# A hybrid decoder layer in float32: a zero-padded bias table, so that bias and row minimum of the attention scores take one instruction instead of two

## The chip, the core and the metric

The kernel runs on one core of a Trainium2 chip. The core has five engines that work side by side, each through a queue of its own: PE (TensorE, matrix products; PEld is its weight load), DVE (VectorE), ACT (ScalarE), POOL (GpSimd) and SP (SyncE, which here issues the transfers). The data lie in SBUF, products of PE land in PSUM. The metric is the device time of one execution in microseconds (us); less is better.

## The reference, cut to what matters

One layer over 1024 positions of 1024 numbers: a norm, one input projection, four mixers side by side (pooling, a short gated convolution, a Conformer convolution, differential attention), an output projection, then a norm and a SwiGLU block of width 2816. The change lies in the attention, which has 4 heads and two maps for each head:

```python
def block(args):
    qblk, start = args
    qpos = start + jnp.arange(Q_BLOCK, dtype=jnp.int32)      # Q_BLOCK = 128
    dist = qpos[:, None] - kpos[None, :]
    bias = rel_bias[rel_bucket(jnp.maximum(dist, 0))]        # 32 buckets
    sc = einsum('bqhmd,bkhmd->bhmqk', qblk, k) * scale + bias
    sc = jnp.where(dist >= 0, sc, NEG_INF)
    p = jax.nn.softmax(sc, axis=-1)
    a = p[:, :, 0] - lam * p[:, :, 1]
    return jnp.einsum('bhqk,bkhd->bqhd', a, v)
```

The bias depends on the distance alone, and from 128 positions back on it is one constant for each head. A constant drops out of the softmax. So only the last 256 columns of a block of 128 rows need a bias (and the mask), measured from that constant; further back it is zero.

## The kernel before, in words

Everything is float32. A product is taken as three matmuls of a high and a low part (mm3, L138 to L140). The program runs through these stages: norm and transpose of x, the input projection with the convolutions on DVE (until about 165 us), projections of K, Q and V (until about 246 us), the scores with the attention (246 to about 400 us), the second norm, and the gate, up and down products to the end.

The attention goes over four pairs of row blocks, p = 0 to 3, and in each over four heads (`unit`). A pair has two blocks i of 128 rows; block i of pair p sees w = 128(2p+1+i) columns, so w runs from 128 to 1024. For each block and each of the two maps m:

- PE writes the negated scores to PSUM, `sc` (L673).
- If w is over 256, DVE takes the minimum over the first w-256 columns into `fmx` (L680). These columns have no bias.
- DVE adds the bias table `tb` to the last 256 columns in place and takes their minimum, with `fmx` as the value to start from, into `mx` (L681, a custom instruction, and a short one that reads its accumulator).
- ACT takes the exponential of mx minus all w columns into `pt`, with the row sums (L684).
- When both maps are there, DVE combines them (L686 to L688).

Then PE transposes the result by blocks into `tp` (L699), ACT and DVE evict it as a high and a low part `at` (L703, L704), and PE multiplies it by V (L708). Other matmuls, those of the output projection for the other mixers (`fm`, L604 to L606), are handed out into gaps of this work by a list of counts (FQ), one entry at each call of `fill1`. Their weights `wo` come through `wsplit`: load, cast to the high part on ACT (L120), low part on POOL (L134).

`tb` (128 x 4 heads x 256) is computed once, from PSUM by two copies on ACT (L461). Its buffer serves again for weights of the gate and up products (`tb2`, loaded by L970).

The order on each engine is not the order of the text: when the program is built, a planner with its own estimates of cost orders the instructions of each engine, by priority and by what is ready. `issue_after` fixes single pairs.

Of the kernel before, what the change touches and what calls it, by code (L numbers as in the profile page):

```python
# [11 lines left out]
F = mybir.dt.float32  # L12
R = mybir.dt.float32r
AF = mybir.ActivationFunctionType
ALU = mybir.AluOpType
AX = mybir.AxisListType
# [3 lines left out]
P = 128  # L20
# [46 lines left out]
def tile_hybrid(ctx, tc, x, norm1_g, w_in, pool_w, pool_scale, sconv_w, conf_w, conf_b, ln_g, ln_b,  # L67
# [3 lines left out]
    V, A, G, T = nc.vector, nc.scalar, nc.gpsimd, nc.tensor  # L71
    dma = nc.sync.dma_start
    x, out, w_in, w_out = x[0], out[0], w_in[0], w_out[0]
# [9 lines left out]
    def pool(name, bufs=1, side="left", **kw):  # L83
        return tc.tile_pool(name=name, bufs=bufs, side=side, reuse_waits="tile", **kw)
# [33 lines left out]
    def cp(e, dst, src):  # L118
        if e == 0:
            A.copy(dst, src)  # L120
        else:
            (V, G)[e - 1].tensor_copy(dst, src)
# [119 lines left out]
    for p in range(4):  # L242
# [16 lines left out]
        h = p // 2  # L259
# [106 lines left out]
    tb = const.tile([P, 4, 256], F, name="tb")  # L366
# [102 lines left out]
    kvp = mid.enter_context(pool("kvp"))  # L469
    VV = [kvp.tile([P, 2, 4, 128], R, name=f"VV{p}") for p in range(4)]  # L470
    qn = [kvp.tile([P, 2, 256], F, name=f"qn{p}") for p in range(4)]

    def proj_tok(c0, use, order=range(4)):
        Ws = [wsplit(w_in[k * 512:(k + 1) * 512, c0:c0 + 256].rearrange("(k p) c -> p k c", p=P), (4,))
              for k in range(2)]
        for p in order:
            ps = ps_mm()
            H = hT[p // 2]
            for i in range(2):
                c = (p % 2) * 256 + i * P  # L480
                o = ps[:, i * 256:(i + 1) * 256]
                for kt in range(8):
                    W = Ws[kt // 4]
                    mm3(o, (H[0][:, kt, c:c + P], H[1][:, kt, c:c + P]), (W[0][:, kt % 4], W[1][:, kt % 4]), kt == 0, kt == 7)
            use(p, ps)
# [99 lines left out]
    def ps_sc():  # L585
        return pss.tile([P, 1024], F, name="sc", tag="sc")

    def ps_tp():
        return psp.tile([P, 512], F, name="tp", tag="tp")

    def ps_av():
        return psq.tile([P, 512], F, name="av", tag="av")
# [48 lines left out]
    def fill1(ins, n=None):  # L641
        for _ in range(next(slots, 0) if n is None else n):
            while fillq:
                f = next(fillq[0], None)
                if f is not None:
                    if GATE:
                        with tc.issue_after(ins.ins):
                            f()
                    else:
                        f()  # L650
                    break
                fillq.pop(0)
# [4 lines left out]
    def unit(u, p, h):  # L657
        if h == 0:
            pend["lt"] = sm.tile([P, 4, 2, 2], F, name="lt", tag="lt", bufs=2)
            pend["o"] = sm.tile([P, 2, 4, 64], F, name="o", tag="kn")  # L660
        lt, o = pend["lt"], pend["o"]
        Ps = []
        for i in range(2):
            w = P * (2 * p + 1 + i)
            nw = min(w, 256)
            pts = [None, None]
            both = ps_sc() if p < 2 else None
            for m in MO:
                hm = 2 * h + m
                sc = ps_sc() if both is None else both[:, 512 * m:512 * m + 512]  # L670
                for c0 in range(0, w, 512):
                    n = min(max(w - c0, 256), 512)
                    ins = T.matmul(sc[:, c0:c0 + n], lhsT=QT[p, h // 2][:, hm % 4, i * P:(i + 1) * P],  # L673
                                   rhs=KT[h // 2][:, hm % 4, c0:c0 + n], start=True, stop=True)
                fill1(ins)
                mx = sm.tile([P, 1], F, name="mx", tag="mx", bufs=4)
                init = 3.0e38
                if w > 256:
                    init = sm.tile([P, 1], F, name="fmx", tag="fmx", bufs=2)
                    V.tensor_reduce(init, sc[:, 0:w - 256], axis=AX.X, op=ALU.min)  # L680
                V.tensor_tensor_reduce(out=sc[:, w - nw:w], in0=sc[:, w - nw:w], in1=tb[:, h, 256 - nw:], scale=1.0,  # L681
                                       scalar=init, op0=ALU.add, op1=ALU.min, accum_out=mx)
                pts[m] = ap4.tile([P, S], F, name="pt", tag=f"pt{m}", bufs=PT1 if m else PT0)
                A.activation(pts[m][:, 0:w], sc[:, 0:w], AF.Exp, bias=mx, scale=-1.0, accum_out=lt[:, h, m, i:i + 1])  # L684
            cf = sm.tile([P, 1], F, name="cf", tag="cf", bufs=4)
            V.reciprocal(cf, lt[:, h, 1, i:i + 1])  # L686
            V.scalar_tensor_tensor(cf, lt[:, h, 0, i:i + 1], nlam, cf, op0=ALU.mult, op1=ALU.mult)
            V.scalar_tensor_tensor(pts[0][:, 0:w], pts[1][:, 0:w], cf, pts[0][:, 0:w], op0=ALU.mult, op1=ALU.add)  # L688
            Ps.append(pts[0])
        if h % 2 == 0:  # L690
            pend["av"] = ps_av()
        avs = pend["av"]
        av = avs[:, (h % 2) * 256:(h % 2) * 256 + 256]
        for kb in range(p + 1):
            ps = ps_tp()
            blocks = [(a, i) for a in range(2) for i in range(2) if 2 * kb + a <= 2 * p + i]
            nb = len(blocks) * P
            for j, (a, i) in enumerate(blocks):
                ins = T.transpose(ps[:, j * P:(j + 1) * P], Ps[i][:, (2 * kb + a) * P:(2 * kb + a + 1) * P], ident)  # L699
            marks.append(ins)  # L700
            fill1(ins)
            at = ap4.tile([P, 2, 512], R, name="at", tag="at", bufs=ATB)
            A.copy(at[:, 0, 0:nb], ps[:, 0:nb])  # L703
            V.tensor_tensor(at[:, 1, 0:nb], ps[:, 0:nb], at[:, 0, 0:nb].bitcast(F), op=ALU.subtract)  # L704
            for s in range(2):
                for a in range(2):
                    n = min(nb - 256 * a, 256)
                    ins = T.matmul(av[:, 256 - n:256], lhsT=VV[kb][:, a, h, :], rhs=at[:, s, 256 * a:256 * a + n],  # L708
                                   start=(kb == 0 and a == 0 and s == 0), stop=(kb == p and a == 1 and s == 1))
                if s == 0:  # L710
                    fill1(ins)
        marks.append(ins)
        fill1(ins)
        if h % 2 == 1:
            oT = sm.tile([P, 512], F, name="oT", tag="sq")
            cp(OTE[u // 2], oT, avs)
            ps = ps_tp()
            for hh in range(2):
                for i in range(2):
                    ins = T.transpose(ps[:, (i * 2 + hh) * P:(i * 2 + hh + 1) * P], oT[:, hh * 256 + i * P:hh * 256 + (i + 1) * P], ident)  # L720
            marks.append(ins)
            fill1(ins)
            psv = ps.rearrange("p (i h d) -> p i h d", i=2, h=2)
            ov = o[:, :, h - 1:h + 1, :]
            cp(OVE[u // 2], ov, psv[:, :, :, 64:128])
            V.tensor_tensor(ov, ov, psv[:, :, :, 0:64], op=ALU.add)
        if h == 3:
            of = o.rearrange("p i h d -> p (i h) d")
            osq = sm.tile([P, 8, 64], F, name="osq", tag="sq")
            A.activation(osq, of, AF.Square)  # L730
            rr = sm.tile([P, 2, 4], F, name="rr", tag="rr", bufs=2)
            rrf = rr.rearrange("p i h -> p (i h)")
            V.tensor_reduce(rrf, osq, axis=AX.X, op=ALU.add)
            l0 = lt[:, :, 0, :]
            l2 = sm.tile([P, 4, 2], F, name="l2", tag="l2", bufs=2)
            V.scalar_tensor_tensor(l2, l0, EPS, l0, op0=ALU.mult, op1=ALU.mult)
            V.scalar_tensor_tensor(rr, rr, 1.0 / 64, l2.rearrange("p h i -> p i h"), op0=ALU.mult, op1=ALU.add)
            G.tensor_tensor(rrf, rrf, mhalf[:, 0:8], op=ALU.pow)
            (G if X5[PO.index(p)] else V).tensor_tensor(qn[p].rearrange("p i (h d) -> p (i h) d", h=4), of, rrf.unsqueeze(2).broadcast_to([P, 8, 64]),
                            op=ALU.mult)  # L740
# [85 lines left out]
    for u in range(16):  # L826
        j, h = u // 4, u % 4
        p = PO[j]
# [355 lines left out]
```

## Time and profile before

| | |
|---|---|
| median of 3 runs | 1082.94 us (1082.12 to 1084.14) |
| the profiled execution: its time, its span | 1081.06 us, 1079.3 us |
| PE busy | 1051.2 us, 97% of the span |
| DVE busy | 732.8 us, 68% |
| ACT busy | 438.9 us, 41% |
| POOL busy | 222.5 us, 21% |
| granted clock of TensorE | 1.000 of full speed |

The span runs from the first to the last instruction. Busy shares are means over the span; what an engine's time is worth differs from stage to stage. A matmul's duration in the trace includes its way through the pipeline, so a PE that is busy all of the time isn't one without any slack.

### The profile page before, as it was taken

How to read it: one execution, taken by the hardware profiler on the slowest of the kernel's cores; microseconds unless marked ns; L12 is line 12 of the kernel's file. 1: busy time of each engine (PE TensorE's matmuls, PEld its weight loads, DVE VectorE, ACT ScalarE, POOL GpSimd, SP SyncE). 2: the span in 40 equal slices, each digit the busy share in tenths (PEclk: the TensorE clock that was granted, in tenths of full speed). 3: DMA queues.
4: the chain of work that ended last, by engine and by line, in shares of the span. 5: the costliest groups of instructions: out<-in, count | busy, mean ns of one | idle time of the engine just before them, and what ended most of it. 6: DMA issues, size and time to landing. Idle time of an engine off the chain costs nothing.

```text
span 1079.3 us, 13508 instructions
## 1 busy us (share of the span) xinstructions
PE 1051.2 (97%) x5203; PEld 875.7 (81%) x5203; DVE 732.8 (68%) x1127; ACT 438.9 (41%) x710; POOL 222.5 (21%) x202
## 2 busy tenths in 40 slices
PE   7999999998989999899999999999999999999998
PEld 7878879996778876788878888888888888888886
DVE  5599984657899966888677675556656567555541
ACT  5512124545786766432332333333333244333320
POOL 5137114655676653000000000000000000000000
PEclk9999999999999999999999999999999999999999
DMA  8131210111021121014576663233223268766721
GB/s 216 49 98 40 59 39 20 40 40 40 30 71 47 50 81 37 14 54 154 210 280 244 250 208 108 73 112 127 88 79 127 106 228 296 246 195 214 231 101 39
DMA packets 89664, 128.04 MB, mean 119 GB/s; under 512 B 17112, under 2 KB 57600, under 8 KB 87040
## 3 DMA queue, kind: packets, MB, share of 16 engines
q1 hardware_dynamic: 89600, 127.18, 36.0%
q8 instruction: 41, 0.67, 0.3%
q14 instruction: 23, 0.19, 0.1%
HBM read 94.13 MB, written 33.04 MB: 118 GB/s over the span
## 4 chain that ended last, share of the span: by engine, by line
PE 81%; DVE 9%; DMA 5%; ACT 2%; issue 1%; POOL 1%; SPq 0%; ACTq 0%; DVEq 0%; POOLq 0%
PE sb L140 10%; PE sb L138 10%; PE sb L139 10%; PE mm L138 6%; PE mm L139 6%; PE mm L140 6%; PE dx L140 3%; PE dx L138 3%; PE dx L139 3%; PE dy L140 3%; PE dy L138 3%; PE dy L139 3%; DMA wd<-in_w_down_dram 2%; DMA dT<-wd 2%; PE fm L606 1%; PE fm L604 1%
## 5 line engine op out<-in xcount | busy, mean ns | idle before, releaser
L138 PE MATMUL sb<-T,rhi 128*128 128x512 f32 x320 | 125.6, 392 | 0.0
L140 PE MATMUL sb<-T,rlo 128*128 128x512 f32 x320 | 125.5, 393 | 0.0
L139 PE MATMUL sb<-T,rhi 128*128 128x512 f32 x320 | 125.5, 392 | 0.0
L911 DVE TENSOR_TENSOR dq<-ds,dq 128x2048 fp32r<-128x2048 f32 x35 | 80.1, 2291 | 60.3 <-ACT dq L910 60.1
L910 ACT CAST dq<-ds 128x2048 fp32r<-128x2048 f32 x35 | 66.8, 1910 | 105.5 <-PE dy L140 39.6
L134 POOL TENSOR_TENSOR wlo<-st,whi 128x1024 fp32r<-128x1024 f32 (+2 forms) x30 | 73.4, 2449 | 113.0 <-ACT whi L120 101.9
L138 PE MATMUL mm<-hT,whi 128*128 128x512 f32 (+1 forms) x224 | 81.0, 373 | 2.4 <-ACT whi L120 1.9
L139 PE MATMUL mm<-hT,whi 128*128 128x512 f32 (+1 forms) x224 | 82.8, 373 | 0.3 <-DVE hT L200 0.2
L140 PE MATMUL mm<-hT,wlo 128*128 128x512 f32 (+1 forms) x224 | 82.1, 370 | 0.0
L317 DVE SCALAR_TENSOR_TENSOR t<-u,cw,t 128x1023 f32<-128x1023 f32 (+28 forms) x58 | 71.4, 1267 | 0.7
L138 PEld LDWEIGHTS sb<-T,rhi 128*128 128x128 f32 x320 | 60.1, 188 | 13.7 <-DVE tp L1030 0.4
L139 PEld LDWEIGHTS sb<-T,rhi 128*128 128x128 f32 x320 | 60.1, 188 | 13.5
L140 PEld LDWEIGHTS sb<-T,rlo 128*128 128x128 f32 x320 | 60.1, 188 | 13.5
L910 ACT CAST rhi<-st 128x1024 fp32r<-128x1024 f32 x28 | 29.4, 1051 | 85.2 <-PE sb L139 46.5
L140 PE MATMUL dx<-dq 128*128 128x512 f32 x160 | 62.4, 390 | 0.0
L139 PE MATMUL dx<-dq 128*128 128x512 f32 x160 | 62.3, 389 | 0.0
L138 PE MATMUL dx<-dq 128*128 128x512 f32 x160 | 61.9, 390 | 0.0
L684 ACT ACTIVATE pt<-sc,mx 128x128 f32<-128x128 f32 (+7 forms) x64 | 47.6, 747 | 18.2 <-DVE mx L681 18.2
L138 PE MATMUL mm<-whi,hT 128*128 128x256 f32 x192 | 54.8, 288 | 0.0
L139 PE MATMUL mm<-wlo,hT 128*128 128x256 f32 x192 | 54.5, 285 | 0.0
L140 PE MATMUL mm<-whi,hT 128*128 128x256 f32 x192 | 54.4, 284 | 0.0
L120 ACT CAST whi<-st 128x1024 fp32r<-128x1024 f32 x28 | 29.4, 1050 | 58.8 <-PE mm L139 52.8
(342 smaller groups left out, 2683.6 us busy)
## 6 DMA issues: line engine op xcount, KB each, us to landing
ds<-dL SPq DMA_DIRECT2D x35, 512.0 KB, 4.0
wd<-in_w_down_dram SPq DMA_DIRECT2D x10, 1024.0 KB, 5.0
dT<-wd SPq DMA_DIRECT2D x10, 1024.0 KB, 4.0
dL<-afs SPq DMA_DIRECT2D x10, 1024.0 KB, 4.4
ds<-dT SPq DMA_DIRECT2D x20, 512.0 KB, 5.4
st<-in_w_in_dram SPq DMA_DIRECT2D x18, 512.0 KB, 3.7
st<-in_w_gate_dram SPq DMA_DIRECT2D x15, 512.0 KB, 4.0
st<-in_w_up_dram SPq DMA_DIRECT2D x15, 512.0 KB, 3.6
```

Of the source, the lines that this page charges most:

```text
L120: A.copy(dst, src)
L134: G.tensor_tensor(lo[:, nv:], st[:, nv:], hi[:, nv:].bitcast(F), op=ALU.subtract)
L138: T.matmul(ps, lhsT=L[0], rhs=Rr[0], start=first, stop=False, skip_group_check=more)
L139: T.matmul(ps, lhsT=L[0], rhs=Rr[1], start=False, stop=False, skip_group_check=more)
L140: return T.matmul(ps, lhsT=L[1], rhs=Rr[0], start=False, stop=last, skip_group_check=more)
L317: V.scalar_tensor_tensor((z if s == 30 else acc)[:, s:], u[:, :S - s], w[:, 30 - s:31 - s], acc[:, s:], op0=ALU.mult, op1=ALU.add)
L604: yield lambda: T.matmul(ps, lhsT=L[0], rhs=Rr[0], start=first, stop=False)
L606: yield lambda: T.matmul(ps, lhsT=L[1], rhs=Rr[0], start=False, stop=last)
L684: A.activation(pts[m][:, 0:w], sc[:, 0:w], AF.Exp, bias=mx, scale=-1.0, accum_out=lt[:, h, m, i:i + 1])
L910: A.copy(hi, src)
L911: (eng or V).tensor_tensor(lo, src, hi.bitcast(F), op=ALU.subtract)
```

## The change

A wider table `tbw` of 7 blocks of 128 columns for each head is made: blocks 0 to 4 are zero (cleared by POOL), blocks 5 and 6 are a copy of `tb` (by ACT). It is laid out by block, then head, then column. Now up to 896 columns take bias and minimum in one instruction. At w = 384 to 896 no L680 is left; at w = 1024 it goes over the first 128 columns. Lines of the changed kernel from here on stand three further down, and then four.

```diff
     qn = [kvp.tile([P, 2, 256], F, name=f"qn{p}") for p in range(4)]
+    tbw = kvp.tile([P, 7, 4, 128], F, name="tbw")
+    G.memset(tbw[:, 0:5], 0.0)
+    A.copy(tbw[:, 5:7].rearrange("p b h n -> p h b n"), tb.rearrange("p h (b n) -> p h b n", b=2))
...
             w = P * (2 * p + 1 + i)
-            nw = min(w, 256)
+            nw = min(w, 896)
...
-                if w > 256:
+                if w > nw:
                     init = sm.tile([P, 1], F, name="fmx", tag="fmx", bufs=2)
-                    V.tensor_reduce(init, sc[:, 0:w - 256], axis=AX.X, op=ALU.min)
-                V.tensor_tensor_reduce(out=sc[:, w - nw:w], in0=sc[:, w - nw:w], in1=tb[:, h, 256 - nw:], scale=1.0,
+                    V.tensor_reduce(init, sc[:, 0:w - nw], axis=AX.X, op=ALU.min)
+                scv = sc[:, w - nw:w].rearrange("p (b n) -> p b n", n=P)
+                V.tensor_tensor_reduce(out=scv, in0=scv, in1=tbw[:, 7 - nw // P:, h, :], scale=1.0,
                                        scalar=init, op0=ALU.add, op1=ALU.min, accum_out=mx)
```

## Rows read from the trace of the kernel before

**Rows 1.** Busy time by stretch: us, then each engine (instructions), clock, DMA

```profile
170.00:180.00 10.00, 10.00 (x87) 10.00 (x86) 4.62 (x11) 4.05 (x9) 3.21 (x2) 1.00 0.01 2
...
280.00:300.00 20.00, 18.39 (x105) 14.85 (x103) 17.73 (x59) 15.22 (x42) 13.53 (x17) 1.00 0.10 31
300.00:320.00 20.00, 17.67 (x104) 14.68 (x102) 19.40 (x47) 16.40 (x37) 13.98 (x13) 1.00 0.21 65
...
340.00:360.00 20.00, 20.00 (x112) 17.35 (x111) 17.90 (x38) 13.20 (x26) 12.98 (x17) 1.00 0.14 41
```

**Rows 2.** Waits from 246 to 410 us: total us, times, longest

```profile
ACT pt L684 <- DVE mx L681: 18.2, 22, 2.1
...
PEld av L708 <- DVE at L704: 5.1, 8, 1.5
```

**Rows 3.** Chain that ended last, from 266 to 340 us: start, us, piece

```profile
279.20 0.53 DVE fmx L680 x2
279.73 0.40 DVE sc L681
...
305.09 1.10 DVE fmx L680 x2
306.18 0.40 DVE sc L681
...
314.65 0.60 DVE fmx L680
```

**Rows 4.** DVE's instructions by line and shape: count, busy, mean ns

```profile
L681 DVE CUSTOM_DVE_ANT_0 sc<-sc,tb,fmx 128x256 f32<-128x256 f32 x48 | 22.4, 485 | 0.1
...
L704 DVE TENSOR_TENSOR at<-tp,at 128x512 fp32r<-128x512 f32 x24 | 16.3, 683 | 3.9 <-ACT at L703 3.9
...
L704 DVE TENSOR_TENSOR at<-tp,at 128x384 fp32r<-128x384 f32 x16 | 8.8, 551 | 2.7 <-ACT at L703 2.7
...
L726 DVE TENSOR_TENSOR o<-o,tp 128x256 f32<-128x256 f32 x8 | 3.3, 414 | 0.0
```

**Rows 5.** DVE in order of time: start us, duration us, line, instruction

```profile
264.37 0.29 DVE L681 CUSTOM_DVE_ANT_0 sc<-sc,tb 128x128 f32<-128x128 f32 x1
...
264.58 0.47 DVE L681 CUSTOM_DVE_ANT_0 sc<-sc,tb 128x256 f32<-128x256 f32 x1
...
266.62 0.27 DVE L680 TENSOR_REDUCE fmx<-sc 128x1 f32<-128x128 f32 x1
266.81 0.41 DVE L681 CUSTOM_DVE_ANT_0 sc<-sc,tb 128x256 f32<-128x256 f32 x1
...
267.15 0.48 DVE L681 CUSTOM_DVE_ANT_0 sc<-sc,tb,fmx 128x256 f32<-128x256 f32 x1
...
356.27 0.95 DVE L680 TENSOR_REDUCE fmx<-sc 128x1 f32<-128x768 f32 x1
357.14 0.41 DVE L726 TENSOR_TENSOR o<-o,tp 128x256 f32<-128x256 f32 x1
```

**Rows 6.** Clearing, cast and table copy: groups by line, and the table's tile

```profile
L387 POOL MEMSET bd<- 128x256 f32 x1 | 0.3, 311 | 0.0
...
L120 ACT CAST whi<-st 128x1024 fp32r<-128x1024 f32 x28 | 29.4, 1050 | 58.8 <-PE mm L139 52.8
...
L461 ACT COPY tb<-mm x2: 585/586/587, 165.3 to 166.2; 128x512 f32<-128x512 f32 x2
```

**Rows 7.** POOL and PE in order of time, from 317 to 328 us

```profile
317.47 1.29 POOL L633 TENSOR_TENSOR x<-x,xr 128x512 f32<-128x512 f32 x1
...
324.12 2.98 POOL L134 TENSOR_TENSOR wlo<-st,whi 128x1024 fp32r<-128x1024 f32 x1 [0.90 <-ACT whi L120]
...
327.15 0.50 PE L605 MATMUL fm<-wlo,sp 128*128 128x512 f32 x1 [0.97 <-POOL wlo L134]
```

**Rows 8.** The table's buffer from 384 us on: its refill and first reader

```profile
L970 SPq DMA_DIRECT2D tb<-in_w_gate_dram x1: 368/368/368, 385.0 to 385.0; - x1
L910 ACT CAST A<-tb x1: 616/616/616, 480.8 to 480.8; 128x512 fp32r<-128x512 f32 x1
```

## Prediction

> **What bounds the kernel now.** I read the table by engine first: the change lies between 266 and 385 us, where the scores are taken, and in the planning ahead of it. [rows 1] give four stretches. At 170 to 180 us PE is busy all of the time (10.00 of 10) and ACT 4.05, POOL 3.21: work that is put there on ACT or POOL is covered by PE. At 280 to 320 us PE has 1.61 and 2.33 us of idle time in 40 us, and DVE is busy 17.73 and 19.40 of 20. At 340 to 360 us PE is busy 20.00 of 20 again, with DVE at 17.90. So the kernel is PE's almost everywhere, but the two middle blocks of the scores (p=1 and p=2) are shared between PE and DVE, and a shorter DVE could be felt there, at most by what PE has idle: 3.94 us.
>
> The waits come second [rows 2]. The largest one of the stage is ACT's exponential waiting for the row minimum: 18.2 us in 22 waits. PE's waits go the other way round, through DVE's eviction of the transposed block (L704): 5.1 us in 8 waits.
>
> The chain that ended last comes third. Between 279 and 319 us it hardly touches PE: it runs through the reduction of the far columns (fmx, L680), bias and minimum (sc, L681) and the exponential [rows 3]. There are eight such places, at 279.20, 282.52, 290.18, 293.42, 300.89, 305.09, 309.67 and 314.65 us. From 327 us on it is a string of matmuls.
>
> **What the change does to DVE.** For each row block of w columns it now takes one instruction over w columns in place of two, L680 over w-256 and L681 over 256. Widths run from 128 to 1024 in steps of 128, eight instances of each (4 heads, 2 maps). At 128 and 256 nothing is joined. At 384 to 896 (40 instances) one instruction goes. At 1024 both stay, the first over 128 and the second over 896.
>
> What counts on a full queue is the distance from start to start, since the rows show that DVE starts an instruction some 0.08 us before the last one ends. From [rows 5]: L680 over 128 columns takes 266.81-266.62 = 0.19 us, over 768 it takes 357.14-356.27 = 0.87, so 0.19 + 0.136 for each further 128. L681 without a start value takes 264.58-264.37 = 0.21 over 128 and 267.15-266.81 = 0.34 over 256: 0.21 + 0.136 for each further 128, within rounding. With a start value (fmx) the piece over 256 takes 0.40 [rows 3], so reading it costs 0.06. Joined: 0.21 + 0.136(n-1) for n blocks; before: 0.19 + 0.136(n-3) + 0.40. The difference is 0.59 - 0.27 - 0.21 = 0.11 us, the same at every width. At 1024: before 0.87 + 0.40 = 1.27, after 0.19 + (0.21 + 0.06 + 6 x 0.136) = 1.28, nothing. Sum on DVE: 40 x 0.11 = 4.4 us.
>
> The Trainium skill (VectorE: DVE Perf Modes, The DRAIN you can't avoid) says that a Vector instruction doesn't start until the pipe of the one before has emptied. Then durations would count and not starts: L680 over 128 takes 0.27, L681 0.48 with and 0.41 without a start value over 256, and the saving would be 0.27 + 0.48 - 0.41 - 0.136 = 0.20 us each, 8 us in all. [rows 5] show starts ahead of ends, so I take 0.11.
>
> The zeros are read through a table with a stride between blocks of 128. No L681 with such an operand is in the trace. The nearest row is L726, which reads and writes 256 columns in blocks of 64: 414 ns, against 683-551 = 132 per 128 of L704, so about 419 for 256 plain columns [rows 4]. Blocks cost nothing there. I take nothing.
>
> **What it adds.** POOL clears 2560 columns: ten times 311 ns at most, 3.1 us. ACT copies 1024 columns: 1.05 us by the cast of that size [rows 6]. The copy can't go before the table is there, at 166.2 + 0.6 us. Both are costed at nothing, because PE is the full engine there [rows 1]. Without that cover they would cost up to 4.2 us, and what queues behind them is evictions on ACT and the weight splits on POOL.
>
> One thing moves: tb is free after that copy and no longer after the last row minimum. Its buffer is filled again by a weight load (L970) that now issues at 385.0 us, right behind that minimum, and is first read at 480.8 [rows 8]. Issued sooner it gains nothing; it is hidden by 95 us already.
>
> **How much of the 4.4 us reaches the end.** At the eight places the scores come in pairs: reduction of a, reduction of b, L681 of a, L681 of b. In the new order a's minimum no longer stands behind b's reduction. Where the chain runs on through both minima to DVE's next instruction (279.20, 314.65) it gains 2 x 0.11 = 0.22 each. Where it leaves through a's exponential, it gains 0.11 plus the whole reduction of b: 0.30 at 282.52 and 290.18 (b over 128), 0.44 at 293.42 (b over 256), 0.57 at 305.09 (b over 384: 1.10 + 0.40 before [rows 3], 0.21 + 5 x 0.136 = 0.89 after, rounded down), 0.71 at 309.67 (b over 512). At 300.89 a's instruction runs while b's scores still come: 0.38. Sum 3.14, and 0.11 more at 379.29: 3.25 us. Bounds: 1.3 if only the plain 0.11 counts at twelve instructions on the chain, 3.9 by PE's idle time. PE is a near second there, so that some of the 3.25 will meet it: I take 80%, 2.6 us. PE's string from 327 us on then starts sooner by that, and the gate, up and down products behind it too, which are PE's.
>
> The profiled execution took 1081.06 us (span 1079.3), 1.88 below the median of the runs shown, 1082.94. Less 2.6: 1078.5 for such an execution, 1080.3 as a median. Own range of this case: 1079.0 to 1081.6. About 0.2% (2.2 us) is what a measurement of this kernel can tell from no change.
>
> **Rivals.**
>
> All of it arrives (chance 0.16). The planner writes each engine's order from its own costs, and with one instruction in place of two, exponentials and evictions can move up also where the chain is PE's now. For it: 18.2 us of waits for the minimum. Against it: PE's 20.00 of 20 from 340 us. It gives the 4.4 us: 1078.5. By the rule of the Trainium skill above (VectorE: DVE Perf Modes, The DRAIN you can't avoid) this rival would give 8 us, 1074.9; the overlapping starts of [rows 5] leave that 0.02 of the 0.16.
>
> Swallowed (0.18). The chain passes 320 to 327 us through a split of output weights on POOL, 324.12 + 2.98 us, for which a matmul waits [rows 7]. Its load waits for a buffer that POOL's L633 frees, 317.47 + 1.29. If POOL's own queue sets that, what DVE gains before 319 is lost there, and 0.11 to 0.5 us is left: 1082.6. Against it: POOL had idle time ahead of these, and what it works on comes from DVE and PE.
>
> Slower (0.16). In the blocks p=2 and p=3 the planner slips an L704 between the two halves, and PE waits for L704 [rows 2]. A joined instruction can't be cut: an eviction behind it waits 0.21 - 0.19 + 2 x 0.136 = 0.29 us longer than behind the reduction alone. There are 12 + 16 = 28 such evictions (of the 24 + 16 in [rows 4]) in these blocks. With all 28 held and PE full it is 28 x 0.29 = 8.1 us, less 3.25: 4.9 slower, 1087.8. It decides from 12 held on, and is slower by over 0.2% from 19 on. For it: PE has nothing idle at 340 to 360 us. Against: fill matmuls stand between. The Trainium skill (Perfetto Trace Analysis, Optimizing Scalar/DVE Operations) has this as a rule: breaking up instructions may let work be completed sooner where Vector makes other engines wait. The 5.1 us of waits for L704 are where this trace bears it out.
>
> The blocks of the table aren't free (0.05). 8 x (3+4+5+6+7+7) = 256 blocks are read; from 4.4/256 = 17 ns a block on, DVE gains nothing. At 40 ns it is 10.2 - 4.4 = 5.8 slower: 1088.7.
>
> **Numbers.** The forecast has 0.45, and it lies on both sides of the 0.2%: faster 0.27, same 0.18. With the 0.16 above, faster is 0.43; swallowed adds 0.18 to same, and a hold of fewer than 19 evictions 0.02, which makes 0.38; slower is 0.14 + 0.05 = 0.19. The range reaches down into the whole saving, 1076.5, and up to 23 of the 28 held evictions (23 x 0.29 - 3.25 = 3.4), 1086.5.
>
> **What would show it.** Forty L680 fewer, and eight left, over 128 columns. L681 over 384 to 896 columns at 0.58 to 1.12 us; 0.2 above that would mean that blocks cost. ACT's wait for the minimum well under 18.2 us. PE's idle time at 280 to 320 us down from 3.94. Copy and clearing somewhere before 200 us with PE still full. PE's waits for L704 over 8 us would show the slower rival. The prediction fails if the planner's new order changes more than these lines do.

## The result, and the profile after

The change makes the kernel slower: 1099.56 us median (1098.68 to 1101.05, 4 runs) against 1083.10 us (1082.12 to 1084.14, now 4 runs), a ratio of 1.0153 with a 95% interval of 1.0130 to 1.0177. That is 16.5 us more, where 2.6 us less were forecast. The profiled execution of the changed kernel took 1100.17 us (span 1098.4, mean granted clock 0.990).

The parts of the change came out as costed. The view by line and shape (count, busy us, mean ns; idle us ahead and what ended it) shows the joined instruction, L685 now, at 581 to 1104 ns over 384 to 896 columns, eight reductions left (L683, 128 columns), and no 256-column instruction that reads `fmx`:

```profile
L685 DVE CUSTOM_DVE_ANT_1 sc<-sc,tbw 128x896 f32<-128x896 f32 x8 | 8.7, 1104 | 1.6 <-PE sc L676 1.6
...
L692 DVE SCALAR_TENSOR_TENSOR pt<-pt,cf 128x768 f32<-128x768 f32 x4 | 6.6, 1662 | 0.0
...
L685 DVE CUSTOM_DVE_ANT_1 sc<-sc,tbw 128x384 f32<-128x384 f32 x8 | 4.6, 581 | 2.1 <-PE sc L676 2.1
...
L683 DVE TENSOR_REDUCE fmx<-sc 128x1 f32<-128x128 f32 x8 | 2.3, 282 | 1.1 <-PE sc L676 1.1
```

Clearing and copy of the wide table run at 166 us, under a full PE (the view of the tile; ns, then start). The first score matmul starts at 246.2 us, 246.3 before:

```profile
L473 POOL MEMSET tbw<- x1: 2238/2238/2238, 166.2 to 166.2; 128x2560 f32 x1
L474 ACT COPY tbw<-tb x1: 1048/1048/1048, 166.7 to 166.7; 128x1024 f32<-128x1024 f32 x1
```

The time goes between the first score and the end of the attention. The same three groups of matmuls in the two traces (durations, then first and last start): the kernel before,

```profile
L673 PE MATMUL sc<-KT,QT x96: 276/389/503, 246.3 to 381.3; 128*128 128x512 f32 x48, 128*128 128x256 f32 x32, 128*128 128x384 f32 x16
L708 PE MATMUL av<-at,VV x160: 217/281/391, 255.5 to 402.9; 128*128 128x256 f32 x128, 128*128 128x128 f32 x32
L138 PE MATMUL sb<-T,rhi x320: 388/392/496, 503.1 to 889.5; 128*128 128x512 f32 x160
```

and the changed one:

```profile
L676 PE MATMUL sc<-KT,QT x96: 274/389/537, 246.2 to 390.2; 128*128 128x512 f32 x48, 128*128 128x256 f32 x32, 128*128 128x384 f32 x16
L712 PE MATMUL av<-at,VV x160: 218/280/581, 256.5 to 417.8; 128*128 128x256 f32 x128, 128*128 128x128 f32 x32
L138 PE MATMUL sb<-T,rhi x320: 389/392/628, 518.1 to 908.6; 128*128 128x512 f32 x160
```

The last score is 8.9 us late, the last product with V 14.9, the first of the later gate and up products 15.0, the last of them 19.1. The stretch from 246 us to the end of the attention holds the same matmuls in both (823 and 822 rows). The view by stretch (us, then busy us and count of PE, PEld, DVE, ACT, POOL, clock, DMA), before and after:

```profile
246.00:403.00 157.00, 146.22 (x823) 120.90 (x821) 137.56 (x354) 110.80 (x258) 99.50 (x98) 1.00 0.17 52
```

```profile
246.00:418.00 172.00, 151.91 (x822) 123.85 (x820) 135.88 (x314) 111.19 (x258) 98.31 (x98) 0.97 0.14 45
```

PE stands idle 172.00 - 151.91 = 20.1 us in place of 157.00 - 146.22 = 10.8: that is 9.3 of the 15 us. The other 5.7 are matmuls that take longer (151.91 us for 146.22), which goes with the mean clock of 0.97. DVE has 40 instructions fewer and is busy only 1.7 us less.

The waits of PE and of its weight loads (total us, times, longest; 246 to 420 us) show what PE stands for. A weight load and the matmul behind it can stand for the same thing at the same time, so the two are not added up. The kernel before,

```profile
PEld sc L673 <- ACT pt L684: 4.6, 12, 1.1
...
PE sc L673 <- ACT pt L684: 1.5, 2, 0.8
```

and the changed one:

```profile
PEld sc L676 <- ACT pt L688: 13.4, 17, 2.6
...
PE sc L676 <- ACT pt L688: 9.1, 10, 2.4
```

A score matmul waits for an exponential when it needs the PSUM buffer that the exponential still reads. ACT's own wait for the minimum, which the forecast had fall "well under 18.2 us", is 19.5 us. PE's loads wait for the eviction (L704, now L708) 5.0 us, 5.1 before [rows 2].

One place shows how: the last two pairs of score matmuls. PE in order of time in the changed kernel,

```profile
383.46 0.40 PE L609 MATMUL fm<-whi,sp 128*128 128x512 f32 x1
385.06 0.73 PE L676 MATMUL sc<-KT,QT 128*128 128x512 f32 x2 [1.21 <-ACT pt L688]
385.62 0.63 PE L712 MATMUL av<-at,VV 128*128 128x256 f32 x4
386.09 0.39 PE L607 MATMUL fm<-whi,sp 128*128 128x512 f32 x1
...
387.04 0.48 PE L712 MATMUL av<-at,VV 128*128 128x256 f32 x2
389.88 0.83 PE L676 MATMUL sc<-KT,QT 128*128 128x512 f32 x2 [2.36 <-ACT pt L688]
390.51 0.52 PE L712 MATMUL av<-at,VV 128*128 128x256 f32 x2
390.83 0.73 PE L607 MATMUL fm<-whi,sp 128*128 128x512 f32 x1
393.07 0.69 PE L712 MATMUL av<-at,VV 128*128 128x256 f32 x2 [1.51 <-DVE at L708]
393.55 0.73 PE L608 MATMUL fm<-wlo,sp 128*128 128x512 f32 x1
394.08 0.63 PE L609 MATMUL fm<-whi,sp 128*128 128x512 f32 x1
```

and before, up to the same pair that starts at 385.06 above:

```profile
376.88 0.34 PE L708 MATMUL av<-at,VV 128*128 128x256 f32 x2
377.07 0.44 PE L605 MATMUL fm<-wlo,sp 128*128 128x512 f32 x1
377.35 0.39 PE L606 MATMUL fm<-whi,sp 128*128 128x512 f32 x1
377.58 0.39 PE L604 MATMUL fm<-whi,sp 128*128 128x512 f32 x1
377.81 0.40 PE L605 MATMUL fm<-wlo,sp 128*128 128x512 f32 x1
378.05 0.39 PE L606 MATMUL fm<-whi,sp 128*128 128x512 f32 x1
378.27 0.40 PE L604 MATMUL fm<-whi,sp 128*128 128x512 f32 x1
378.52 0.74 PE L673 MATMUL sc<-KT,QT 128*128 128x512 f32 x2
```

Before, six fill matmuls stand right ahead of this pair, and the exponential is done when PE gets there. In the changed kernel a single one does: PE halts 1.21 us, and the fill matmuls that could have run stand behind the scores in the same queue. At the next pair PE halts 2.36 us, but that halt is not the order's alone. The exponential is late there because ACT stands at a cast of output weights that waits for its transfer:

```profile
387.78 1.04 ACT L120 CAST whi<-st 128x1024 fp32r<-128x1024 f32 x1 [2.77 <-DMA st<-in_w_out_dram]
```

Behind the halt PE's clock is granted at 0.54 and then 0.78 of full speed, so that for much of these 10 us it was at the lower of its two levels, 1.2 in place of 2.4 GHz:

```profile
385.00:390.00 5.00, 2.58 (x15) 2.12 (x16) 3.42 (x8) 2.23 (x5) 1.10 (x1) 1.00 0.15 54
390.00:395.00 5.00, 3.49 (x11) 2.56 (x12) 4.36 (x7) 2.39 (x5) 1.27 (x1) 0.54 0.33 105
395.00:400.00 5.00, 5.00 (x29) 4.39 (x27) 2.65 (x5) 3.59 (x7) 3.22 (x2) 0.78 0.00 0
```

So the planner laid out the stage anew. Compared as lists, 110 of PE's 5196 instructions moved against the others (67 of DVE's 1015, 43 of ACT's 632, 8 of POOL's 200). Of PE's, 54 are score matmuls that stand earlier, by up to 36 places, and 15 are transposes into `tp` that stand later.

### The profile page after: what moved, and what is told of

The parts are those of the page before. It is cut to its first block, busy times and chain, and to the rows that moved or that the text cites. A ratio compares the mean times of both kernels' runs of the same rounds, so it can differ in the third digit from the quotient of the medians.

```text
span 1098.4 us, 13474 instructions
## 1 busy us (share of the span) xinstructions
PE 1057.7 (96%) x5203; PEld 878.1 (80%) x5203; DVE 731.4 (67%) x1087; ACT 440.6 (40%) x711; POOL 223.8 (20%) x203
## 4 chain that ended last, share of the span: by engine, by line
PE 76%; DVE 10%; DMA 7%; ACT 3%; issue 2%; POOL 1%; SPq 0%; ACTq 0%; DVEq 0%; POOLq 0%
PE sb L138 9%; PE sb L140 9%; PE sb L139 9%; PE mm L139 6%; PE mm L140 6%; PE mm L138 6%; PE dx L138 3%; PE dx L140 3%; PE dx L139 3%; DMA wd<-in_w_down_dram 3%; DMA dT<-wd 3%; PE dy L138 2%; PE dy L139 2%; PE dy L140 2%; PE fm L609 1%
## 5 line engine op out<-in xcount | busy, mean ns | idle before, releaser
L134 POOL TENSOR_TENSOR wlo<-st,whi 128x1024 fp32r<-128x1024 f32 (+2 forms) x30 | 72.3, 2414 | 121.1 <-ACT whi L120 110.0
L688 ACT ACTIVATE pt<-sc,mx 128x896 f32<-128x896 f32 (+7 forms) x64 | 47.6, 746 | 23.9 <-DVE mx L685 19.5
```

Of the source, the lines that this page charges most:

```text
L134: G.tensor_tensor(lo[:, nv:], st[:, nv:], hi[:, nv:].bitcast(F), op=ALU.subtract)
```

## The experiments

Each ratio is against runs of the kernel before that were taken beside the experiment (11 to 24 of them, medians from 1080.98 to 1082.87 us). Brackets hold the 95% interval.

**First four: is it the work, or the order?** The theory after the traces is that the work is as costed and the new order on PE costs the time. Its rivals are the wide table (its operand or its upkeep) and the long instruction itself. Where an order is held, each engine's instructions are chained in a stored order for the planner, without a wait on the chip; the table's clearing and copy stay free.

```diff
         tile_hybrid(tc, *args)
+        replay(tc, SKIP)   # for each engine: add_manual_dep(b, a.name, NoSync) along ORD[engine]
```

`table_only` keeps the two instructions and reads the last 256 columns through the wide table:

```diff
-            nw = min(w, 896)
+            nw = min(w, 256)
```

> Only the wide table: cleared, copied and read through its stride, with 256 columns at most in one instruction, two instructions as before. Its order on PE, VectorE, ScalarE and GpSimd is that of the kernel before; one load, the refill of the narrow table's buffer, is issued sooner. Theory 'order' and theory 'joined instruction' both expect 1083 us, within 1.5. A rival 'table' (clearing, copy, early load or the strided operand cost the 16 us) expects 1095 us and more.

Measured: 1083.44 us (10 runs), ratio 1.0009 [0.9996, 1.0022]. PE, DVE, ACT and POOL have exactly the order of before here. Table, clearing, copy, strided operand and the earlier refill of `tb` cost nothing that can be told (at most 2.4 us, by the interval).

`join_old_order`: the changed kernel, all five engines in the order of before.

> The changed kernel with all its instructions, but queued on every engine in the order that the kernel before has (the clearing and the copy of the table are free). Theory 'order': the joined instructions cost what was forecast (0.58 to 1.12 us), and the 16 us come from the planner's new order alone; then this is at or below the kernel before, near the 1080.3 us of the forecast, 1078.5 to 1083. Rival 'joined instruction': longer instructions on VectorE hold other work whatever the order; then it stays near 1099 us, above 1092 at least.

Measured: 1082.48 us (10 runs), 1.0009 [0.9995, 1.0023]. The same work is 1.4%, some 16 us, faster in the old order than in the new one. But the forecast's 2.6 us don't show either: they would be a ratio of 0.9976, below the interval.

`split_new_order`: `table_only`, so with the two instructions again, and all engines in the order of the changed kernel (each reduction right ahead of its L681).

> The wide table is there but the reduction and the 256-column instruction are two again, as in the kernel before, queued in the order of the changed kernel, each reduction right ahead of its second half. Theory 'order': slow like the changed kernel or slower by the 4.4 us of VectorE time that the split costs, 1099 to 1104 us. Rival 'joined instruction': back near 1083 us.

Measured: 1102.65 us (4 runs), 1.0188 [1.0173, 1.0204]. The order alone costs 20 us. Within it, joining saves 3.1 us by the medians (1102.65 - 1099.56); the intervals of the two ratios overlap a little.

`join_old_pe`: only PE's order is held, the others are planned freely.

> The changed kernel with only TensorE's queue held to the order of the kernel before; the planner orders the other engines. Against the kernel before, 42 of VectorE's and 22 of ScalarE's instructions stand elsewhere. If it is TensorE's new order that costs (scores queued ahead of the release of their buffer), 1080 to 1086 us. If it is the order on VectorE or ScalarE, 1090 us and more.

Measured: 1084.40 us (7 runs), 1.0023 [1.0007, 1.0040]. PE's order, with the other engines planned around it, is 1.0153 - 1.0023 = 1.3%, 14 of the 16.5 us.

**Two sides of PE's order.** `sc_held` ties each score matmul behind the other matmul that it followed before; `sc_advanced_free` does the reverse, the others in the old order and the scores at their new places.

```diff
+        hold(tc)   # sc_held: for each score matmul a, add_manual_dep(a, b.name, NoSync), b = what it followed before
```

> After with one rule more for the planner: each score matmul stays behind the other matmul behind which it stood in the kernel before (order only, no wait); everything else is planned as in after. Theory A (the score matmuls stand up to 36 places sooner, in front of the exponentials that free their PSUM buffers, and PE stands there): the waits of PE and its loads for exponentials fall from 22 us to under 9, and the time to 1081 to 1087 us. Theory B (it is the later transposes and av products, or the order of DVE and ACT, that cost): the time stays at 1093 us or more.

Measured: 1087.52 us (4 runs), 1.0063 [1.0042, 1.0084]. Its chart of waits from 246 to 420 us has, for PE's loads, 5.5 us where the changed kernel has 13.4 (PE itself 2.2 in place of 9.1), and ACT's wait for the minimum is down to 14.8:

```profile
ACT pt L703 <- DVE mx L700: 14.8, 15, 2.1
...
PEld sc L691 <- ACT pt L703: 5.5, 12, 1.1
```

The time is 0.5 us above what theory A gave, but far from B: 0.9%, 10 us, comes back from the places of the scores. In this kernel 39 instructions of PE and 76 on the other engines still stand as the planner put them; the 6.5 us that remain are somewhere in those and were not split further.

> The other half: PE's other matmuls stand in the order of before, and only the score matmuls are put in the places that they have in after; the other engines are planned freely. Theory A (the places of the score matmuls alone cost the time): 1093 to 1101 us, with PE's waits for exponentials over 15 us. Theory B (the others' order costs it): 1081 to 1088 us.

Measured: 1095.41 us (4 runs), 1.0133 [1.0107, 1.0160]. Its waits for exponentials:

```profile
PEld sc L698 <- ACT pt L710: 9.8, 16, 1.6
...
PE sc L698 <- ACT pt L710: 5.6, 8, 1.4
```

The places of the scores, with DVE and ACT planned around them, bring 14 us. So both sides say that the places of the scores are most of the loss. The profiled execution was the slowest of the four (1100.54 us), and its waits for exponentials are still less than in the changed kernel; PE's loads wait 7.8 us for the eviction, 5.1 before. So the loss here is not in waits for exponentials alone.

**Does the time follow the joining?** `join_512` joins up to 512 columns, so that 16 of the 40 reductions go, and is planned freely.

```diff
-            nw = min(w, 896)
+            nw = min(w, 512)
```

> After with at most 512 columns joined in one instruction (nw = min(w, 512)), in the planner's own order. Theory A (any change of the lengths on DVE makes the planner lay out the scores anew, and the time follows the layout and not the saving): a time that does not follow the number of joined instructions (16 of 40 dropped, half of the saving or less would be 1 to 2 us), anything from 1079 to 1103 us, and in step with PE's waits for exponentials. Theory B (the long joined instruction itself makes PE wait): 1084 to 1092 us, between before and after, as half of the columns are held back.

Measured: 1092.81 us (4 runs), 1.0119 [1.0092, 1.0145]; waits for exponentials 3.9 and 7.0 us. Four tenths of the joining bring over seven tenths of the loss, and the time is 0.8 us over B's bound. It doesn't tell the theories far apart, but no proportion is seen. Its order is also a different one: counted by the other matmuls ahead of them, only 4 of the 96 score matmuls stand earlier than before, by at most 5, and 33 stand later. So a new order can lose 1.2% without early scores. PE's loads wait 7.8 us for the eviction here too; what costs in this kernel was not split.

**Where are the 2.6 us in the old order?** `join_early` puts the joined instruction where the reduction stood (38 of 40; the tile `mx` got 8 buffers in place of 4, for its longer life).

> The order of before on all engines, as in the run of the old order, but the joined instruction stands where the reduction of the far columns stood (38 of 40), one to a few places sooner on DVE, so that a's minimum no longer stands behind b's reduction. Theory A (my forecast of 2.6 to 3.25 us by sooner exponentials holds once the order is kept): 1078.5 to 1080 us, ACT's wait for the minimum under 14 us. Theory B (what DVE saves is given back by the collision of DVE's second addition with POOL's split of the output weights near 323 us, or on PE's string from 327 us on): 1081.5 to 1084 us.

Measured: 1087.54 us (6 runs), 1.0069 [1.0045, 1.0094]. Against both theories. ACT waits for the minimum 10.6 us in 10 waits, as A had it, yet the kernel is slower. Set matmul by matmul against the trace before, it gains 1.2 us from 260 to 318 us, has lost 0.5 of it by 333, and (besides a halt near 580 us) falls back by 0.1 us in every 10 from 510 to 885 us, where nothing was changed: there PE does less in the same busy time. The last run below follows that up.

In `join_old_order` the same comparison gives 0.9 us gained from 264 to 318 us and 2.2 lost from 322 to 336. The first large step is an addition of two SBUF tiles on DVE (`pt`, L688) against POOL's split of weights (L134). Before, the addition starts ahead of the split [rows 7]:

```profile
323.98 0.88 DVE L688 SCALAR_TENSOR_TENSOR pt<-pt,cf 128x640 f32<-128x640 f32 x1
```

in `join_old_order` the split is ahead by 0.04 us (lines stand 26 further down):

```profile
323.86 3.03 DVE L718 SCALAR_TENSOR_TENSOR pt<-pt,cf 128x640 f32<-128x640 f32 x1
...
323.82 2.38 POOL L160 TENSOR_TENSOR wlo<-st,whi 128x1024 fp32r<-128x1024 f32 x1 [0.91 <-ACT whi L146]
```

The one that starts second ends last: 2.98 us for POOL in the first, 3.03 us for DVE in the second. Two kernels change just this pair of places on DVE; each stands in the old order otherwise.

```diff
  # join_old_swap, DVE's stored order      # before_collide, DVE's stored order
-  joined sc (768), pt (640)               -  pt (640), at (384)
+  pt (640), joined sc (768)               +  at (384), pt (640)
```

> The joined instruction in the order of before, with one pair changed on DVE: the addition of the two maps near 323 us (640 columns) stands ahead of the joined instruction before it, so that it starts near 323.0 us and ends before POOL's split of the output weights starts (323.8 us). Theory A (that addition took 3.03 us in place of 0.88 because the split had started 0.04 us ahead of it): it takes 0.9 to 1.0 us, the step of 1.9 to 2.5 us behind 322 us is gone against the run of the old order, and the time is 1080 to 1081.5 us, 0.5 to 1.5 under the kernel before. Theory B (the saving is swallowed by PE's string or the split itself): the same as before within 0.15%.

> The kernel before with one pair changed on DVE: the same addition stands behind the eviction that follows it, so that it starts near 324.5 us, after POOL's split (324.1 us) has started. Theory A (whichever of the two starts first holds the other up): the addition takes 2.3 to 3.0 us in place of 0.88, the split 2.4 in place of 2.98, and the program is 1 to 2 us slower, 1083 to 1084.5 us. Theory B (the stretched addition had another cause): it takes 0.9 us, and the time does not change.

Measured: `join_old_swap` 1082.16 us (12 runs), 0.9997 [0.9983, 1.0011]; `before_collide` 1082.39 us (12 runs), 1.0005 [0.9992, 1.0018]. The addition, then the split, in the one and in the other:

```profile
321.49 0.89 DVE L718 SCALAR_TENSOR_TENSOR pt<-pt,cf 128x640 f32<-128x640 f32 x1
...
322.22 2.39 POOL L160 TENSOR_TENSOR wlo<-st,whi 128x1024 fp32r<-128x1024 f32 x1 [0.92 <-ACT whi L146]
```

```profile
324.94 2.27 DVE L714 SCALAR_TENSOR_TENSOR pt<-pt,cf 128x640 f32<-128x640 f32 x1
...
324.13 2.40 POOL L160 TENSOR_TENSOR wlo<-st,whi 128x1024 fp32r<-128x1024 f32 x1 [0.90 <-ACT whi L146]
```

The collision is as theory A says: it can be taken away and put in. In `before_collide` PE is 1.25 us late from 330 us on. The median times are those of theory B, though the intervals (1.8 us under to 1.2 over, and 0.9 under to 1.9 over) don't exclude the 1 us of A. In the traces the lag is gone by 555 us, but that is no absorbing: the kernel before halts at 549 us in its one profiled execution (62 matmuls are at work from 540 to 555 us, 67 in `before_collide`), and `join_old_swap`, which comes to 540 us at the same time as the kernel before, gains 0.8 us there as well. And `join_old_swap`, 2.1 us ahead of the trace before at 318 us (1.15 of it from ahead of the scores), still loses 1.2 us from 325 to 336. It loses 1.6 more near 378, of which all but 0.6 is back by 390 us. At 378 ACT's cast of output weights waits for its transfer, the exponential stands behind it, and PE halts for that 1.4 us:

```profile
377.39 1.05 ACT L146 CAST whi<-st 128x1024 fp32r<-128x1024 f32 x1 [1.66 <-DMA st<-in_w_out_dram]
378.34 1.00 ACT L714 ACTIVATE pt<-sc,mx 128x896 f32<-128x896 f32 x1
```

`table_only`, with the old work in the old order, has the same halt there, 1.1 us, and so has the changed kernel (its 2.36 us above). The wait is not set by the order: in `join_best` and `join_best_256` below, which have the same queues and are both 1.3 us behind the trace before at 377 us, this cast waits 2.29 and 0.41 us.

`join_best` is `join_old_swap` with seven joined instructions at the places of their reductions, those on the chain of the forecast. Compared as lists, though, DVE's queue differs from that of `join_old_swap` in two instructions only: an addition (L756) and a reciprocal (L716) now come behind the joined one. With joined instructions the old order, too, has no reduction of b in front of a's minimum any more.

> The run with the changed pair, and beside it seven of the eight joined instructions on the chain moved up to the places of their reductions (at 300.89 us to the later one's place it can't be done alone), so that a's minimum comes sooner, as my forecast had it. Theory A (the forecast's 2.6 us are there once the order is kept and the collision avoided): 1078.5 to 1080 us. Theory B (sooner exponentials on these places give little, PE is the near second): 1080 to 1081.5 us, as the run with the changed pair alone.

Measured: 1088.06 us (7 runs), 1.0042 [1.0019, 1.0065], and it falls back from 600 us on as `join_early` does. The two share one thing that the others don't have: `mx` has 8 buffers, by which everything that is laid out behind it in SBUF, the operands of the gate, up and down products among it, lies 128 bytes further on (h2b at 44160 in place of 44032).

```diff
-                mx = sm.tile([P, 1], F, name="mx", tag="mx", bufs=8)
+                mx = sm.tile([P, 1], F, name="mx", tag="mx", bufs=12)
```

> The same as the run with the early joined instructions, but the little mx tile has 12 buffers in place of 8, so that everything behind it in SBUF lies 256 bytes further than in the kernel before, and not 128. Theory A (the 128 bytes made the gate and up products slower: 1210 matmuls between 600 and 880 us in place of 1226, all with a full PE): 1222 to 1230 matmuls there, and 1080.5 to 1083 us. Theory B (sooner joined instructions cost 4 to 6 us by themselves): 1210 matmuls or the loss elsewhere, and 1086 us or more. By my forecast's own mechanism, with the 2.6 us, it would be 1080.3 us or less.

Measured: 1081.63 us (12 runs), 0.9995 [0.9977, 1.0013]. From 600 to 880 us, `join_best` and then `join_best_256`, both at the full clock:

```profile
600.00:880.00 280.00, 280.00 (x1210) 227.89 (x1209) 166.66 (x221) 95.73 (x133) 0.00 (x0) 1.00 0.37 129
```

```profile
600.00:880.00 280.00, 280.00 (x1226) 229.76 (x1225) 168.68 (x223) 97.81 (x135) 0.00 (x0) 1.00 0.37 132
```

Theory A's 1226 matmuls, to the count. With the layout set right the two sooner minima cost nothing, and gain nothing that can be told: the 1080.3 us of the forecast lie 1.3 below the median, and the interval reaches from 2.5 us under before to 1.4 over. No version is shown to beat the kernel before.

## Why the prediction was wrong

**The step that failed** is the first sentence of "How much of the 4.4 us reaches the end" and all behind it: every price was put on the order of before, with forty instructions taken out of it. The prediction named the condition, "the prediction fails if the planner's new order changes more than these lines do", and gave it no rival, no price and no chance. It changed 110 places on PE and 118 on the other engines, and the new order is the whole loss: 1082.48 us with the order held, 1099.56 without. The range ended at 1086.5.

**What the order does** is shown by `sc_held` (10 us back) and `sc_advanced_free` (14 us lost): score matmuls stand in the queue before the exponentials that free their PSUM buffers are done, with the fill matmuls behind them. The waits, 9.1 us of PE for exponentials in place of 1.5, fit that. Why the planner put them there was not tried. A guess is that its estimates follow the shorter work on DVE, while FQ hands out the fills by counts that fitted the old order.

**DVE's saving was sized right, and its share on the chain too high.** The joined starts follow the forecast (0.87 us from start to start over 768 columns; 0.21 + 5 x 0.136 = 0.89). Starts lie ahead of the ends here too, by about 0.08 us, so the 8 us don't fit these rows. They were worked out from a rule of the Trainium skill (VectorE: DVE Perf Modes, The DRAIN you can't avoid); the same section of the Trainium skill adds that an instruction that is not held starts earlier, and that is what the rows show. 3.1 us are the most that a pair of medians here shows, in the new order. In the old order the forecast's 3.25 us on the chain came to 0.9 (`join_old_order`) and 1.2 us (`join_early`) by 318 us. That sum is the mis-sized term: under four tenths of it had arrived at 318 us, ahead of the steps told next.

**The 2.6 us at the end** were not there, as the rival "swallowed" had it, though by other steps than its own. POOL's split at 324 us was one place, not by its queue but by the addition that it held up. Without that, `join_old_swap` still gives back 1.2 us by 336 us. Near 325 us DVE waits 0.68 us for a V product there, a gap in which the kernel before ran the reduction of 512 columns, so that half of a pair can be a filler; no run took this apart. The transfer near 378 us is no part of the change. These shares are read from one trace each, and `table_only`, with the work and the order of before, falls behind it by 0.9 us within the attention; so how the 2.6 us divide stays open. With the order held, "same" is what was measured.

**The rival "slower"**, evictions held behind the long instruction, is not what happened in the changed kernel: PE's loads wait 5.0 us for them, where "over 8 us" was to show it, and `join_old_order` has the long instructions at no loss. (In `sc_advanced_free` and `join_512` those waits are 7.8 us, near that sign.) So the direction was right in that rival, by luck, and its mechanism wrong. "Blocks of the table" is excluded by `table_only` and by 581 to 1104 ns.

**Copy, clearing and refill** were hidden as costed; `table_only` shows it.

**A second loss in the profiled execution** is no part of the change. Between 575 and 600 us, 19.1 - 15.0 = 4.1 us are added: DVE's queue waits for a load of the down weights that took 7.4 us, PE's next product waits 2.6 us behind it, and the clock is granted at 0.66 from 595 to 600 us. `table_only` has 2.4 us of the same wait. Why that load takes 5 us in one execution and over 7 in another stays open.

## What to carry to other kernels

Where a planner orders the queues, an edit's price has two terms, the work and the new order, and the second can be several times the first. So hold the old order (a stored order as edges without waits), time the edit that way before its own worth is judged, and give "the order changes" a rival with a price. In an in-order queue, what matters for PE is not how soon a matmul is queued but what stands behind it when its buffer is still held: keep independent fills ahead of it. And a lag read from two single traces is worth no more than what two traces of the same work and order differ by, here about 1 us within the attention.

## What the runs showed that was not expected

**128 bytes of SBUF.** Four small buffers more moved the operands of the gate and up products by 128 bytes, and PE did 1210 matmuls in 280 us in place of 1226, 231.4 ns each against 228.4, at the full clock. Another 128 bytes further on it was gone. That is 1.3% on these products and 6.4 us between the medians (1088.06 - 1081.63; 5 us by the ratios, 1.0042 - 0.9995), for an edit that touches none of them. Which operand's place decides was not tried.

**DVE and POOL hold each other up** where a DVE instruction reads two SBUF tiles while POOL reads SBUF: 3.03 us for 0.88, or 2.98 for 2.38, depending on which starts some 0.1 us sooner. The Trainium skill (SBUF — State Buffer, SBUF: two separate sides) says that the one that starts first keeps the shared ports for its whole instruction and the other blocks; the three pairs of rows above that overlap by more than 0.2 us agree. The joined instruction, whose one operand lies in PSUM, was not held up: in `join_old_swap` it took 0.96 us over 768 columns in the middle of a split, and 959 ns is the mean of the changed kernel. What a new order changes is which additions are caught: in the changed kernel the four over 768 columns take 1662 ns on the mean, 1126 before, but those over 1024 columns 1392, 1739 before. Over all widths the additions take 31.4 us, 31.5 before.

**The clock** fell behind halts of PE in the changed kernel (0.54 of full speed from 390 to 395 us, behind 2.36 us). But it also fell near 254 us in most of the kernels and not in others with the same queue up to there. From 240 to 260 us it was 0.91 in the changed kernel and in `join_old_order`, and 1.00 before and in `table_only`. That costs up to 1.1 us and follows no edit here.
